# A two-layer hybrid trunk in split fp32: later and larger loads in the down products, their differences on VectorE, and small constants made later

## The chip, the cores and the metric

The kernel runs on one core of a Trainium2 chip. The metric is the device time of one execution in microseconds. The engines are TensorE (PE; its weight loads are listed as PEld), VectorE (DVE), ScalarE (ACT), GpSimd (POOL) and SyncE (SP), which issues every DMA in one ordered queue. Each engine works through its own instructions in the order in which the program lists them, and waits there for semaphores of the others.

## The reference, cut to what matters

Two layers, sequence and width 1024, a hidden width of 4096, all in float32. Layer 0 mixes by dilated window attention, layer 1 by a gated linear recurrence (HGRN2).

```python
def reference(x, ...):
    lbs = forget_lower_bounds(lb_logits)          # softmax and cumulative sum over layers, for HGRN2
    for i in range(2):
        y = dilated_attention_mixer(x, ...) if i == 0 else hgrn2_mixer(x, ..., lbs[i])
        x = layer_norm(ALPHA * x + y, ln_mix_g[i], ln_mix_b[i])
        y = jnp.square(jax.nn.relu(x @ ffn_w_up[i])) @ ffn_w_down[i]     # up: 1024x4096, down: 4096x1024
        x = layer_norm(ALPHA * x + y, ln_ffn_g[i], ln_ffn_b[i])
    return x
```

## The kernel before

**Products.** A float32 operand is split into a high and a low part (`split`: ACT copies it into the type fp32r that PE multiplies, DVE subtracts this from the operand to get the low part), and every product is high x high + high x low + low x high: three matmuls of 128x128 by 128x512. Large products are done in a scheme of the Strassen kind with seven block products instead of eight, numbered i = 1 to 7; each needs sums or differences of blocks as operands and is added to some of the output blocks.

**Stages in time**, by the trace: attention to about 1040 us, its output product and LayerNorm to 1100, up product of layer 0 to 1433, down product to 1768, HGRN2 to 2130, its output product to 2220, up product of layer 1 to 2544, down product to 2866, and the last LayerNorm.

**Up product.** It writes seven left operands for the down product (`hd[i - 1, j]`, 16 tiles of 128x512 each) to DRAM: the squared ReLU of the blocks and their sums S1 to S4. In the last pair of rows these sums (`upa` to `upd`, lines L1131 to L1146) stand on DVE between the first splits of the down product.

**Down product (in `ffn`).** `steps` lists (i, j, quarters): the block products in the order 1, 6, 7, 5, 4, 2, each of 16 steps j, and in each step 12 matmuls (four quarters of 128 rows, three matmuls each). Block product 3 comes last and in three passes over its 16 steps: quarters 0 and 1, then quarter 2, then quarter 3, so that LayerNorm of finished rows runs beside the rest. A turn of the loop calls `load_down(n + 8)`, `product_down(n)`, `split_down(n + 2)` and `after(n)`, which adds results and issues pieces of LayerNorm. Instructions of this loop are placed by a scheduler; a split may stand at most five steps ahead of its product (`HOLD`).

- `load_down` fetches the left tile (`hd`) and, where needed, the right block (`w_down`), 256 KB each, into one slot `dr` of 512 KB; the `U` pool has 50 such slots. For i = 1 three tiles come: left, `top[:, L]`, and `top[:, R]` into `held(3, j)`.
- `split_step` makes the parts `dS` (left) and `dT` (right). The right operands of later products are differences. They are made ahead in the slots `held(n, j)`: POOL makes `held(1, j)` in i = 1 (L1213), the difference of i = 4 in place (L1215), and one of two in i = 6 (L1222); DVE makes the other (L1223).
- In block product 3 the left tile is `d3`, 128x256 or 128x128, loaded step by step into the three buffers of a small pool (tag `p`); its parts are `d3s`, again in three buffers.

**LayerNorm** works on `z`: statistics and scaling on DVE and ACT, an add of the bias on POOL (L212) in layer 0, and in layer 0 a store to `x3d` and transposes on PE (L221).

**Attention.** Turn n multiplies `H` (split weights) with `xh`, `xl` (split x transposed; also its differences xT). Eviction is `e`, L685 on. At n = 11 `constants()` also loads and copies `bsel` (L451), which is read first by the mixing of head groups, near 270 us. `hgrn_consts()` comes in the program behind the attention's output product; its instructions (names `hc_`, 28 on DVE of 128x8) need only `lb_logits`, and the scheduler puts them at the very start.

Of the kernel before, what the change touches and what calls it, by code (L numbers as in the profile page):

```python
# [9 lines left out]
F32 = mybir.dt.float32  # L10
# [33 lines left out]
HOLD = 5  # L44
LOADDN = 8
SPLITDN = 2
LOADW = 8
SPLITW = 5
UNIT0 = 3
# [11 lines left out]
def trunk_kernel(  # L61
# [72 lines left out]
    def split(raw, hi, lo):  # L134
        act(hi, raw, AF.Copy)  # L135
        nc.vector.tensor_sub(lo, raw, hi.bitcast(F32))  # L136
# [180 lines left out]
        return t  # L317


    def attention(pre):  # L320
        cosT = U("cosT")
        sinT = U("sinT")
        units = [(pr, g) for pr in range(NPAIR) for g in GORD]
# [121 lines left out]
        def constants():  # L445
            nc.sync.dma_start(cosT, cos_t)
            nc.sync.dma_start(sinT, sin_t)
            nc.sync.dma_start(mask, masks)
            selw = wp.tile([P, 512], F32, name="selw", tag="p")[:, :NG * P]
            nc.sync.dma_start(selw, bsel)  # L450
            act(sel, selw, AF.Copy)  # L451
            nc.gpsimd.memset(frow.bitcast(F32), 0.0)
# [304 lines left out]
        for n in range(len(seq)):  # L757
            gi, i, j = seq[n]
            load_w(n + LOADW)
            if j == 0 and n // 3 < 6:  # L760
                get_T(n // 3 + 1, 1)
            if j == 1 and n // 3 >= 5:
                get_T(n // 3 + 2, 0)
            if j == 2 and n // 3 >= 5:
                get_T(n // 3 + 2, 1)
            if n == 11:
                constants()
            if n == len(seq) - 2 * PREA - 3:
# [12 lines left out]
            if n % 21 == 14:  # L781
                last = gi == len(groups) - 1
                base = n + 7
                work = [unit_work(gi, a, base) for a in range(2)]
                for a in range(2):
                    adds, rope_of, core, stats, mix = work[a]
                    steps = [f for t in range(2) for f in (lambda rope_of=rope_of, t=t: rope_of(t),
                                                           lambda adds=adds, t=t: adds[t][0](),
                                                           lambda adds=adds, t=t: adds[t][1]())]
                    if last:  # L790
                        both = [lambda f=f: (f[0](), f[1]()) for f in (steps[1:3], steps[4:6])]
                        tail.append(([steps[0], both[0], steps[3], both[1]], core, stats, mix))
                        continue
                    for k, f in zip(ROPES[a], steps):
                        at(base + k, f)
                    for k, f in enumerate(core):
                        at(base + UNIT0 + OFFS[a][k], f)
                    for k, f in zip(STATS[a], stats):
                        at(base + k, f)
                    for k, f in zip(MIX[a], mix):  # L800
                        at(base + k, f)
                if last:
                    for a in range(2):
                        for k, f in list(zip(ROPES0[a], tail[a][0])):
# [202 lines left out]
    def ffn(li, xf, late, res, gB_ap, bB_ap, last, pre=None):  # L1007
# [146 lines left out]
        rows_, ops, hold, keepT = {}, {}, {}, {}  # L1154

        def held(n, j):
            if (n, j // 2) not in hold:
                hold[n, j // 2] = U("hold")
            return hold[n, j // 2][:, (j % 2) * 512:(j % 2) * 512 + 512]

        def load_down(n):
            if n >= len(steps):
                return
            i, j, qs = steps[n]
            top, bot = w_down[li, j], w_down[li, j + NP]
            if i == 3:
                c = slice(qs[0] * P, (qs[-1] + 1) * P)
                t = wp.tile([P, 512], F32, name="d3", tag="p")[:, :len(qs) * P]
                nc.sync.dma_start(t, hd[i - 1, j][:, c])
                r = None  # L1170
                if qs == PASS[0]:
                    r = U("dr3")[:, L]
                    nc.sync.dma_start(r, bot[:, R])
                rows_[n] = t, r
                return
            two = U("dr")
            t, r = two[:, L], two[:, R]
            nc.sync.dma_start(t, hd[i - 1, j])
            if i == 1:
                nc.sync.dma_start(r, top[:, L])  # L1180
                nc.sync.dma_start(held(3, j), top[:, R])
# [7 lines left out]

        def split_down(n):  # L1190
            if n >= len(steps):
                return
            first = len(nc.cur_bb.bb.instructions)
            split_step(n)
            if n - HOLD in begun:
                for i in list(nc.cur_bb.bb.instructions)[first:]:
                    tc.add_manual_dep(i, begun[n - HOLD], mybir.DependencyInfo(
                        mybir.DependencyClass.NoSync, mybir.DependencyReason.DATA), reason="hold")

        def split_step(n):  # L1200
            i, j, qs = steps[n]
            t, r = rows_.pop(n)
            if i == 3:
                w = len(qs) * P
                S_ = wp.tile([P, 512], F32R, name="d3s", tag="pts")[:, :2 * w]
                split(t, S_[:, 0:w], S_[:, w:2 * w])
                if r is not None:
                    keepT[j] = parts_of(r, "dT3")
                ops[n] = S_, keepT[j]
                return  # L1210
            S_ = parts_of(t, "dS")
            if i == 1:
                g.tensor_sub(held(1, j), held(3, j), r)  # L1213
            elif i == 4:
                g.tensor_sub(r, r, held(2, j))  # L1215
            elif i == 5:
                r = held(1, j)
            elif i == 7:
                r = held(3, j)
            elif i == 6:  # L1220
                t1, t2, t3 = held(1, j), held(2, j), held(3, j)
                g.tensor_sub(t2, r, t1)  # L1222
                v.tensor_sub(t3, r, t3)  # L1223
                r = t2
            ops[n] = S_, parts_of(r, "dT")

        cur = {}

        def product_down(n):
            i, j, qs = steps[n]  # L1230
            S_, T_ = ops.pop(n)
# [6 lines left out]
            w = len(qs) * P  # L1238
            for n_, q in enumerate(qs):
                h, l = S_[:, n_ * P:(n_ + 1) * P], S_[:, w + n_ * P:w + (n_ + 1) * P]  # L1240
                nc.tensor.matmul(o[q], h, T_[:, L], start=begin, stop=False, skip_group_check=True)  # L1241
                if n not in begun:
                    begun[n] = list(nc.cur_bb.bb.instructions)[-1].name
                nc.tensor.matmul(o[q], h, T_[:, R], start=False, stop=False, skip_group_check=True)  # L1244
                nc.tensor.matmul(o[q], l, T_[:, L], start=False, stop=end, skip_group_check=True)  # L1245
# [129 lines left out]
        for n in range(len(steps)):  # L1375
            load_down(n + LOADDN)
            product_down(n)
            split_down(n + SPLITDN)
            after(n)
        order.__exit__()  # L1380
        return xn, []
# [78 lines left out]
    def hgrn(xs, late, consts, pre, gw):  # L1460
# [101 lines left out]
        for hd in range(8):  # L1562
# [61 lines left out]
            for i in range(3):  # L1624
# [15 lines left out]
    oN, fill = attention(pr.pre_steps)  # L1640
    xf, late = outproj_ln(pr, oN, fill, lambda t: x[t * P:(t + 1) * P, :],
                          ln_mix_g[0], ln_mix_b[0], x1d)
    hc = hgrn_consts()
    gw = GateW()
    xs, late = ffn(0, xf, late, x1d, ln_ffn_g[0], ln_ffn_b[0], False, lambda: gw.prefetch(0))
    pr = Out(w_hgrn_out, "h", 1)
# [81 lines left out]
```

## Time and profile before

| | |
|---|---|
| Times of three runs | 2872.73, 2873.05, 2877.30 us; median 2873.05 |
| Profiled execution | 2876.54 us, of which the span from first to last instruction is 2874.7 |
| Mean granted PE clock | 0.993 of full speed |
| Busy | PE 2797.4 us (97%), DVE 2085.0 (73%), ACT 1453.8 (51%), POOL 306.0 (11%) |
| DMA engines | 51% busy, 485 MB moved |
| POOL, line L1213 | 32 subtractions of 128x512, 56.3 us, 1767 ns each |
| DVE, line L136, dS | 192 low parts of 128x512, 169.6 us, 883 ns each |

Rows of a timeline give start, duration, engine, line, operation, written and read tiles, shapes, and in brackets how long the engine had stood idle and what released it. Rows of waits give the waiting engine and line, what it waited for, the sum in us, how often, and the longest. Rows of windows give, for a stretch, its length, the busy time and instructions of PE, PEld, DVE, ACT and POOL, the granted clock, the DMA engines' share and GB/s. Starts count from the first instruction.

### The profile page before, as it was taken

What the parts mean: (1) busy time and instruction counts of PE and PEld (TensorE: products, weight loads), DVE (VectorE), ACT (ScalarE), POOL (GpSimd) and SP (SyncE); (2) the same over time, 40 slices, a digit from 0 to 9 for tenths busy, and PEclk for the clock granted to TensorE, in tenths of its full rate; (3) what the DMA queues carried; (4) which work ended last, traced back from release to release, by engine and by line L of the source; (5) the groups of instructions that cost most, each with busy time, mean ns of one, the idle gap of its engine ahead of it and who ended that gap; (6) DMA issues with size and microseconds to landing.
All of it is one profiled execution on the core that took longest, in us unless ns stands there. A gap on an engine that the chain in (4) does not pass through costs nothing. (4 is left out here: it accounts for less than half of the span.)

```text
span 2874.7 us, 40257 instructions
## 1 busy us (share of the span) xinstructions
PE 2797.4 (97%) x14152; PEld 2235.7 (78%) x14152; DVE 2085.0 (73%) x3766; ACT 1453.8 (51%) x3137; POOL 306.0 (11%) x163
## 2 busy tenths in 40 slices
PE   7999999999999989999999999999999999999998
PEld 6777777777777767888878886778877788878885
DVE  7768777777787777786696786564667687678776
ACT  5555555555555455544444445454553644444433
POOL 0000000000000003000160511110101200042400
PEclk9999999999999999999999999999999999999999
DMA  7766665666667423564574733001132365484643
GB/s 269 264 199 192 192 198 176 207 217 199 198 200 222 134 80 143 172 216 145 204 254 144 259 123 121 30 30 59 59 118 103 127 220 177 147 315 148 221 159 113
DMA packets 206218, 485.28 MB, mean 169 GB/s; under 512 B 30656, under 2 KB 44992, under 8 KB 206016
## 3 DMA queue, kind: packets, MB, share of 16 engines
q1 hardware_dynamic: 206016, 482.72, 51.0%
q8 instruction: 111, 1.82, 0.3%
q14 instruction: 91, 0.75, 0.1%
HBM read 362.82 MB, written 94.24 MB: 159 GB/s over the span
## 5 line engine op out<-in xcount | busy, mean ns | idle before, releaser
L662 PE MATMUL pmm<-xh,H 128*128 128x512 f32 x1008 | 407.4, 404 | 16.0 <-ACT H L430 9.2
L664 PE MATMUL pmm<-xh,H 128*128 128x512 f32 x1008 | 395.8, 393 | 1.0 <-DVE H L438 1.0
L663 PE MATMUL pmm<-xl,H 128*128 128x512 f32 x1008 | 395.5, 392 | 0.0
L662 PEld LDWEIGHTS pmm<-xh,H 128*128 128x128 f32 x1008 | 190.8, 189 | 56.1 <-ACT H L430 9.2
L664 PEld LDWEIGHTS pmm<-xh,H 128*128 128x128 f32 x1008 | 190.1, 189 | 43.3 <-DVE H L438 1.7
L663 PEld LDWEIGHTS pmm<-xl,H 128*128 128x128 f32 x1008 | 190.8, 189 | 36.7
L510 ACT ACTIVATE p<-p,stats 128x128 f32<-128x128 f32 (+1 forms) x384 | 168.4, 442 | 99.9 <-DVE stats L507 99.5
L1241 PE MATMUL pdy<-dT,dS 128*128 128x512 f32 x512 | 199.2, 389 | 0.0
L1244 PE MATMUL pdy<-dT,dS 128*128 128x512 f32 x512 | 199.2, 389 | 0.0
L1245 PE MATMUL pdy<-dT,dS 128*128 128x512 f32 x512 | 199.2, 389 | 0.0
L212 POOL TENSOR_TENSOR z<-z,bB 128x1024 f32<-128x1024 f32 x24 | 58.6, 2444 | 1294.5 <-ACT z L211 1287.7
L136 DVE TENSOR_TENSOR dS<-dr,dS 128x512 fp32r<-128x512 f32 x192 | 169.6, 883 | 12.2 <-ACT dS L135 12.2
L135 ACT ACTIVATE dS<-dr 128x512 fp32r<-128x512 f32 x192 | 120.0, 625 | 111.6 <-PE pdy L1245 43.7
L507 DVE CUSTOM_DVE_ANT_0 p<-s,mask 128x128 f32<-128x128 f32 (+1 forms) x384 | 113.6, 348 | 66.0 <-PE s L496 58.4
L169 PE MATMUL pmm<-f0nh,wh 128*128 128x512 f32 x384 | 153.2, 399 | 0.7 <-ACT wh L135 0.7
L171 PE MATMUL pmm<-f0nh,wl 128*128 128x512 f32 x384 | 149.9, 390 | 0.0
L170 PE MATMUL pmm<-f0nl,wh 128*128 128x512 f32 x384 | 149.7, 390 | 0.0
L1213 POOL TENSOR_TENSOR hold<-hold,dr 128x512 f32<-128x512 f32 x32 | 56.3, 1767 | 548.8 <-DMA hold<-in_w_down_dram 540.3
L523 ACT ACTIVATE pts<-ppt 128x256 f32<-128x256 f32 (+1 forms) x192 | 85.5, 474 | 56.9 <-PE ppt L520 55.1
L1065 ACT ACTIVATE H<-wc 128x512 fp32r<-128x512 f32 x128 | 77.2, 625 | 73.3 <-DVE wc L1058 44.0
L136 DVE TENSOR_TENSOR dT<-dr,dT 128x512 fp32r<-128x512 f32 x128 | 111.4, 875 | 2.5 <-ACT dT L135 1.8
L1244 PEld LDWEIGHTS pdy<-dT,dS 128*128 128x128 f32 x512 | 96.1, 188 | 20.0
(395 smaller groups left out, 7133.4 us busy)
## 6 DMA issues: line engine op xcount, KB each, us to landing
xh<-xtd SPq DMA_DIRECT2D x110, 512.0 KB
xl<-xtd SPq DMA_DIRECT2D x110, 512.0 KB
dr<-hd SPq DMA_DIRECT2D x192, 256.0 KB
dr<-in_w_down_dram SPq DMA_DIRECT2D x160, 256.0 KB
rot<-e SPq DMA_DIRECT2D x192, 128.0 KB
wa<-in_w_up_dram SPq DMA_DIRECT2D x48, 512.0 KB
wb<-in_w_attn_dram SPq DMA_DIRECT2D x36, 512.0 KB
wa<-in_w_attn_dram SPq DMA_DIRECT2D x33, 512.0 KB
```

Of the source, the lines that this page charges most:

```text
L135: act(hi, raw, AF.Copy)
L136: nc.vector.tensor_sub(lo, raw, hi.bitcast(F32))
L169: nc.tensor.matmul(o, wh[:, k], xs.h(k), start=k == 0, stop=False)
L170: nc.tensor.matmul(o, wh[:, k], xs.l(k), start=False, stop=False)
L171: nc.tensor.matmul(o, wl[:, k], xs.h(k), start=False, stop=k == NK - 1)
L510: act(p[:, h, :n], p[:, h, :n], AF.Exp, bias=sS[:, 0, h, b:b + 1], scale=-1.0, accum_out=sS[:, 1, h, b:b + 1])
L662: nc.tensor.matmul(o, wh, hi[k // 2][:, c], start=begin and k == 0, stop=False, skip_group_check=True)
L663: nc.tensor.matmul(o, wh, lo[k // 2][:, c], start=False, stop=False, skip_group_check=True)
L664: nc.tensor.matmul(o, wl, hi[k // 2][:, c], start=False, stop=end and k == 3, skip_group_check=True)
L1241: nc.tensor.matmul(o[q], h, T_[:, L], start=begin, stop=False, skip_group_check=True)
L1244: nc.tensor.matmul(o[q], h, T_[:, R], start=False, stop=False, skip_group_check=True)
L1245: nc.tensor.matmul(o[q], l, T_[:, L], start=False, stop=end, skip_group_check=True)
```

## The change

It has three parts. In the down products the right block `top[:, R]` of i = 1 is loaded with step j + 4, and the subtractions of POOL go to DVE. The left tiles of block product 3 come in loads of 512 KB into `U` slots (four steps of pass 1, eight of passes 2 and 3), and in passes 2 and 3 one split of 256 columns serves two steps and is issued up to four steps ahead. In attention, the bsel part of `constants()` moves from n = 11 to n = 30 and `hgrn_consts()` to n = 36, where DVE's and PE's orders are those of the program.

```diff
+SPLIT3 = 4
+SHIFT = 4
...
-        def constants():
...
+        def constants2():
             selw = wp.tile([P, 512], F32, name="selw", tag="p")[:, :NG * P]
             nc.sync.dma_start(selw, bsel)
             act(sel, selw, AF.Copy)
...
+            if n == 30:
+                constants2()
+            if n == 36:
+                hc.append(hgrn_consts())
...
             top, bot = w_down[li, j], w_down[li, j + NP]
+            if 0 <= n - SHIFT < NP:
+                nc.sync.dma_start(held(3, n - SHIFT), w_down[li, n - SHIFT][:, R])
             if i == 3:
-                t = wp.tile([P, 512], F32, name="d3", tag="p")[:, :len(qs) * P]
-                nc.sync.dma_start(t, hd[i - 1, j][:, c])
+                w = len(qs) * P
+                js = 1024 // w
+                if j % js == 0:
+                    many[qs] = U("d3")
+                    nc.sync.dma_start(many[qs].rearrange("p (j c) -> p j c", c=w),
+                                      hd[i - 1, j:j + js, :, qs[0] * P:qs[0] * P + w].rearrange("j p c -> p j c"))
+                t = many[qs][:, j % js * w:min(j % js * w + 256, 1024)]
...
             if i == 1:
-                nc.sync.dma_start(r, top[:, L])
-                nc.sync.dma_start(held(3, j), top[:, R])
+                nc.sync.dma_start(held(1, j), top[:, L])
...
-                S_ = wp.tile([P, 512], F32R, name="d3s", tag="pts")[:, :2 * w]
-                split(t, S_[:, 0:w], S_[:, w:2 * w])
+                S_ = wp.tile([P, 512], F32R, name="d3s", tag="pts")
+                split(t, S_[:, 0:256], S_[:, 256:512])
...
+                if len(qs) == 1:
+                    rows_.pop(n + 1)
+                    ops[n + 1] = S_[:, P:256], S_[:, 256 + P:512], keepT[j + 1]
...
             if i == 1:
-                g.tensor_sub(held(1, j), held(3, j), r)
+                r = held(1, j)
             elif i == 4:
-                g.tensor_sub(r, r, held(2, j))
+                v.tensor_sub(r, r, held(2, j))
...
-                g.tensor_sub(t2, r, t1)
+                v.tensor_sub(t2, r, t1)
...
+            if 0 <= n - SHIFT + 1 < NP:
+                a = n - SHIFT + 1
+                v.tensor_sub(held(1, a), held(3, a), held(1, a))
...
+            if n + SPLIT3 < len(steps) and len(steps[n + SPLIT3][2]) == 1:
+                split_down(n + SPLITDN + 1)
+                split_down(n + SPLIT3)
...
+    hc = []
+    oN, fill = attention(pr.pre_steps, hc)
...
-    hc = hgrn_consts()
+    hc = hc[0]
```

How this moves instructions shows at three places (numbers behind names tell buffers apart; the new kernel's lines are 2 to 22 higher). ACT at the start, before: two splits of an x block (`xh_157`, `xh_158`), the copy of bsel, the splits of xT2, the first eviction.

```order
9 L135 ACTIVATE xh_157<-x11_110 128x1024
10 L135 ACTIVATE xh_158<-x11_112 128x1024
11 L451 ACTIVATE bsel_95<-selw_415 128x384
12 L135 ACTIVATE xh_173<-xT2_169 128x1024
13 L135 ACTIVATE xh_174<-xT2_170 128x1024
14 L685 ACTIVATE e_194<-pmm_181 128x512
15 L430 ACTIVATE H_196<-wa_108 128x512
```

And in the changed kernel:

```order
9 L137 ACTIVATE xh_157<-x11_110 128x1024
10 L137 ACTIVATE xh_158<-x11_112 128x1024
11 L137 ACTIVATE xh_173<-xT2_169 128x1024
12 L137 ACTIVATE xh_174<-xT2_170 128x1024
13 L689 ACTIVATE e_194<-pmm_181 128x512
14 L432 ACTIVATE H_196<-wa_108 128x512
```

The copy of bsel has left this place, and nothing has come in. The second place is DVE at the seam of layer 0's up and down products, before: the up product's last sums (`upb`, `upd`, `upc`, `upa`) among the first splits of the down product.

```order
2120 L1131 TENSOR_TENSOR upb_13290<-pup_13370,upc_13338 128x512
2121 L136 TENSOR_TENSOR dS_13392<-dr_13244,dS_13392 128x512
2122 L136 TENSOR_TENSOR dT_13397<-dr_13244,dT_13397 128x512
2123 L1137 TENSOR_TENSOR upd_13412<-pup_13348,upb_13290 128x512
2124 L1146 TENSOR_TENSOR upd_13412<-upa_13262,upd_13412 128x512
2125 L136 TENSOR_TENSOR dS_13422<-dr_13273,dS_13422 128x512
2126 L136 TENSOR_TENSOR dT_13426<-dr_13273,dT_13426 128x512
2127 L1146 TENSOR_TENSOR upc_13338<-upd_13412,upc_13338 128x512
2128 L1146 TENSOR_TENSOR upb_13290<-upc_13338,upa_13262 128x512
2129 L1146 TENSOR_TENSOR upa_13262<-upb_13290 128x512
2130 L136 TENSOR_TENSOR dS_13456<-dr_13297,dS_13456 128x512
2131 L136 TENSOR_TENSOR dT_13461<-dr_13297,dT_13461 128x512
```

In the changed kernel (L1245 is the subtraction that POOL made; `hold_13339` holds the right blocks that are loaded later):

```order
2120 L1139 TENSOR_TENSOR upb_13288<-pup_13367,upc_13334 128x512
2121 L138 TENSOR_TENSOR dS_13390<-dr_13244,dS_13390 128x512
2122 L138 TENSOR_TENSOR dT_13393<-hold_13246,dT_13393 128x512
2123 L1145 TENSOR_TENSOR upd_13408<-pup_13345,upb_13288 128x512
2124 L1245 TENSOR_TENSOR hold_13246<-hold_13339,hold_13246 128x512
2125 L1154 TENSOR_TENSOR upd_13408<-upa_13261,upd_13408 128x512
2126 L138 TENSOR_TENSOR dS_13418<-dr_13272,dS_13418 128x512
2127 L138 TENSOR_TENSOR dT_13421<-hold_13246,dT_13421 128x512
2128 L1154 TENSOR_TENSOR upc_13334<-upd_13408,upc_13334 128x512
2129 L1245 TENSOR_TENSOR hold_13246<-hold_13339,hold_13246 128x512
2130 L1154 TENSOR_TENSOR upb_13288<-upc_13334,upa_13261 128x512
2131 L1154 TENSOR_TENSOR upa_13261<-upb_13288 128x512
```

Two subtractions stand in the chain of sums and splits, and the third step's `dS` and `dT` follow in the next two rows. The same triple `dS`, `dT`, L1245 repeats for the steps behind. The third place is SP in the last block product of layer 1, before: loads of quarter tiles among the stores of the finished rows.

```order
1402 L1169 DMA d3_25033<-hd1_86 128x128
1403 L209 DMA out_0_dram<-z_23846 128x512 x2
1404 L1169 DMA d3_25041<-hd1_86 128x128
1405 L1169 DMA d3_25049<-hd1_86 128x128
1406 L1169 DMA d3_25073<-hd1_86 128x128
1407 L209 DMA out_0_dram<-z_23848 128x512 x2
1408 L1169 DMA d3_25081<-hd1_86 128x128
```

In the changed kernel, passes 2 and 3 together:

```order
1341 L1181 DMA d3_24765<-hd1_86 128x8x128
1342 L1181 DMA d3_24859<-hd1_86 128x8x128
1343 L1181 DMA d3_24913<-hd1_86 128x8x128
1344 L1181 DMA d3_24968<-hd1_86 128x8x128
1345 L211 DMA out_0_dram<-z_23718 128x512 x2
1346 L211 DMA out_0_dram<-z_23720 128x512 x2
1347 L211 DMA out_0_dram<-z_23722 128x512 x2
```

All four loads stand ahead of the stores. In layer 0 they do not: SP has there, in the changed kernel,

```order
893 L1181 DMA d3_15806<-hd0_85 128x8x128
894 L1181 DMA d3_15900<-hd0_85 128x8x128
895 L1296 DMA x3d_89<-z_14719 128x1024
896 L1296 DMA x3d_89<-z_14721 128x1024
897 L1181 DMA d3_15997<-hd0_85 128x8x128
898 L1181 DMA d3_16087<-hd0_85 128x8x128
```

where the last two are those of pass 3, behind the stores of two rows of `z` to `x3d`.

More of the change, by code (lines that the diff above doesn't have):

```diff
@@ L317, in parts_of, with attention @@
         return t
-    def attention(pre):
+    def attention(pre, hc):
         cosT = U("cosT")
@@ L1153, in ffn @@
         steps += [(3, j, qs) for qs in PASS for j in range(NP)]
-        rows_, ops, hold, keepT = {}, {}, {}, {}
+        rows_, ops, hold, keepT, many = {}, {}, {}, {}, {}
         def held(n, j):
@@ L1165, in load_down @@
             top, bot = w_down[li, j], w_down[li, j + NP]
+            if 0 <= n - SHIFT < NP:
+                nc.sync.dma_start(held(3, n - SHIFT), w_down[li, n - SHIFT][:, R])
             if i == 3:
-                c = slice(qs[0] * P, (qs[-1] + 1) * P)
-                t = wp.tile([P, 512], F32, name="d3", tag="p")[:, :len(qs) * P]
-                nc.sync.dma_start(t, hd[i - 1, j][:, c])
+                w = len(qs) * P
[5 more added lines that the diff above has]
+                t = many[qs][:, j % js * w:min(j % js * w + 256, 1024)]
                 r = None
@@ L1191, in split_down @@
             if n >= len(steps):
+                return
+            if n in ops:
                 return
@@ L1203, in split_step @@
             if i == 3:
-                w = len(qs) * P
-                S_ = wp.tile([P, 512], F32R, name="d3s", tag="pts")[:, :2 * w]
-                split(t, S_[:, 0:w], S_[:, w:2 * w])
+                S_ = wp.tile([P, 512], F32R, name="d3s", tag="pts")
+                split(t, S_[:, 0:256], S_[:, 256:512])
                 if r is not None:
                     keepT[j] = parts_of(r, "dT3")
-                ops[n] = S_, keepT[j]
+                ops[n] = S_[:, 0:256], S_[:, 256:512], keepT[j]
+                if len(qs) == 1:
+                    rows_.pop(n + 1)
+                    ops[n + 1] = S_[:, P:256], S_[:, 256 + P:512], keepT[j + 1]
                 return
@@ L1221, in split_step @@
                 t1, t2, t3 = held(1, j), held(2, j), held(3, j)
-                g.tensor_sub(t2, r, t1)
+                v.tensor_sub(t2, r, t1)
                 v.tensor_sub(t3, r, t3)
                 r = t2
-            ops[n] = S_, parts_of(r, "dT")
+            ops[n] = S_[:, L], S_[:, R], parts_of(r, "dT")
+            if 0 <= n - SHIFT + 1 < NP:
+                a = n - SHIFT + 1
+                v.tensor_sub(held(1, a), held(3, a), held(1, a))
         cur = {}
@@ L1230, in product_down @@
             i, j, qs = steps[n]
-            S_, T_ = ops.pop(n)
+            sh, sl, T_ = ops[n]
             if j == 0 and i in (1, 5):
@@ L1237, in product_down @@
             begin, end = j == 0 and i in (1, 5, 6, 2), j == NP - 1 and i in (1, 2, 3, 4)
-            w = len(qs) * P
             for n_, q in enumerate(qs):
-                h, l = S_[:, n_ * P:(n_ + 1) * P], S_[:, w + n_ * P:w + (n_ + 1) * P]
+                h, l = sh[:, n_ * P:(n_ + 1) * P], sl[:, n_ * P:(n_ + 1) * P]
                 nc.tensor.matmul(o[q], h, T_[:, L], start=begin, stop=False, skip_group_check=True)
@@ L1639, in trunk_kernel @@
     pr = Out(w_attn_out, "a", 0)
-    oN, fill = attention(pr.pre_steps)
+    hc = []
+    oN, fill = attention(pr.pre_steps, hc)
     xf, late = outproj_ln(pr, oN, fill, lambda t: x[t * P:(t + 1) * P, :],
                           ln_mix_g[0], ln_mix_b[0], x1d)
-    hc = hgrn_consts()
+    hc = hc[0]
     gw = GateW()
```

## The prediction

> **What bounds the kernel now.** I read the busy times first.
>
> ```profile
> PE 2797.4 (97%) x14152; PEld 2235.7 (78%) x14152; DVE 2085.0 (73%) x3766; ACT 1453.8 (51%) x3137; POOL 306.0 (11%) x163
> ```
>
> TensorE (PE) is busy for 97% of the 2874.7 us span, and the change leaves its instructions alone. Time can therefore come only from the 77 us in which PE is idle and from stretches at a lower clock. The idle stretches and their waits, read next, lie in three places that the edits touch: the start, the first steps of both down products, and the last product of both.
>
> The timeline of the start (start, us, engine, in brackets the idle time and its releaser):
>
> ```profile
> 19.38 2.35 DVE L349 TENSOR_TENSOR xT<-x,xT 128x1024 f32<-128x1024 f32 x2
> ...
> 23.87 0.52 ACT L451 ACTIVATE bsel<-selw 128x384 fp32r<-128x384 f32 x1 [8.12 <-DMA selw<-in_bsel_dram]
> ...
> 24.30 1.99 ACT L135 ACTIVATE xh<-xT 128x1024 fp32r<-128x1024 f32 x2
> ...
> 26.19 0.58 ACT L685 ACTIVATE e<-pmm 128x512 f32<-128x512 f32 x1
> ...
> 26.82 0.80 PE L662 MATMUL pmm<-xh,H 128*128 128x512 f32 x1 [6.82 <-ACT e L685]
> 27.41 0.63 PE L663 MATMUL pmm<-xl,H 128*128 128x512 f32 x1
> ...
> 30.40 0.63 PE L664 MATMUL pmm<-xh,H 128*128 128x512 f32 x1
> ```
>
> ScalarE (ACT) works in order. Its copy of bsel waits 8.12 us for a small load; the splits of xT and the eviction e stand behind it, and PE waits 6.82 us for e. After that pause matmuls follow at (30.40 − 27.41)/7 = 0.427 us.
>
> The windows by stage give, left to right, PE, weight load, VectorE (DVE), ACT and GpSimd (POOL), then clock, DMA share and rate. The rows are the down product's first product (i=1), its second (i=6) and third (i=7) in layer 0:
>
> ```profile
> 1433.40:1482.80 49.40, 46.23 (x191) 36.85 (x192) 47.58 (x46) 22.49 (x39) 38.92 (x20) 0.97 0.98 354
> 1482.80:1526.30 43.50, 43.50 (x193) 36.02 (x192) 36.73 (x47) 22.35 (x41) 13.04 (x8) 1.00 0.33 102
> 1526.30:1569.80 43.50, 43.50 (x193) 36.02 (x193) 24.93 (x41) 19.17 (x33) 0.00 (x0) 1.00 0.50 152
> ```
>
> All hold the same 192 matmuls. i=6 and i=7 take 43.5 us with PE full; i=1 takes 49.4, so 5.9 us are lost, and there DVE is busy for 47.58 us with only 46 instructions. Its timeline tells why:
>
> ```profile
> 1436.14 0.69 DVE L1146 TENSOR_TENSOR upd<-upa,upd 128x512 f32<-128x512 f32 x1 [1.36 <-ACT upd L1094]
> ...
> 1436.27 1.72 POOL L1213 TENSOR_TENSOR hold<-hold,dr 128x512 f32<-128x512 f32 x1 [0.94 <-DMA hold<-in_w_down_dram]
> ...
> 1436.75 1.78 DVE L136 TENSOR_TENSOR dS<-dr,dS 128x512 fp32r<-128x512 f32 x1
> ...
> 1439.04 1.85 POOL L1213 TENSOR_TENSOR hold<-hold,dr 128x512 f32<-128x512 f32 x1 [1.06 <-DMA hold<-in_w_down_dram]
> ...
> 1439.77 1.67 DVE L1146 TENSOR_TENSOR upb<-upc,upa 128x512 f32<-128x512 f32 x1
> ...
> 1442.09 0.69 DVE L136 TENSOR_TENSOR dS<-dr,dS 128x512 fp32r<-128x512 f32 x1
> ...
> 1442.69 0.68 DVE L136 TENSOR_TENSOR dT<-dr,dT 128x512 fp32r<-128x512 f32 x1
> ...
> 1443.43 0.50 PE L1244 MATMUL pdx<-dT,dS 128*128 128x512 f32 x1 [1.90 <-DVE dT L136]
> ```
>
> A DVE instruction that meets a POOL subtraction takes 1.67 to 1.78 us, and one that meets none 0.68 to 0.69; back to back they start 0.60 apart (1442.09, 1442.69). PE waits for the end of this DVE chain, the low part dT of the third step.
>
> **The change part by part.**
>
> *Start.* Both small-constant blocks leave. The two xT splits can now begin while DVE makes xT (its two subtractions end at 19.38 + 2.35 = 21.73). The second split takes half of 1.99 us, 1.0, then e 0.58: PE resumes at 23.4 instead of 26.8, a gain of **3.4 us**. A pause of 3.4 us is left, and I keep the slow clock behind it (the layer-1 rows below show it after 1.39 us idle). Without it 8 to 10 matmuls gain 0.2 each, 2.1 at most, so the bounds are 2.5 and 5.5.
> The Trainium skill (TensorE: Matmul & The Clock Gate, Part 1) lets the clock fall after an idle window of about 3.4 us, which runs free. By that rule the shorter pause may keep full speed; the 1.39 us below speak against it.
>
> *The block at product 36.* It is 28 DVE instructions of this size in one run, with three waits for ACT between:
>
> ```profile
> L1404 DVE TENSOR_TENSOR hc_e<-hc_e,hc_den 128x8 f32<-128x8 f32 x2 | 0.2, 162 | 0.0
> ...
> L1402 DVE RECIPROCAL hc_den<-hc_den 128x8 f32<-128x8 f32 x1 | 0.2, 197 | 0.0
> 107.00:152.00 45.00, 44.74 (x267) 34.49 (x266) 29.02 (x76) 28.41 (x83) 0.00 (x0) 1.00 0.61 195
> ```
>
> 28 x 0.165 = 4.6 us, 0.7 for the copy of cm, and up to a microsecond for each wait: 6 to 9 us in which the evictions' subtractions, the score work L507 and the weights' low parts H queue on DVE. Products 30 to 40 have PE full (44.74 of 45.00) and DVE at 29.02, so 16 us are free and the block fits, but in one piece. I take **+0.5**, bounds 0 and 4. The bsel load and copy at product 30 have no reader nearby: 0.
>
> *First product of the down products.* The ACT copies that start the chain (upd, 1436.14) do not move. In the new order nine DVE instructions run from there to the low part dT of the third step: upd, dS, dT, upc, one subtraction, upb, upa, dS, dT. Eight starts 0.60 apart and the last at 0.68 end at 1436.14 + 4.8 + 0.7 = 1441.6, and PE goes 0.06 later: 1441.7 instead of 1443.43, **1.7 us**. The other new subtraction there falls into DVE's idle 1.36. Layer 1 has the same chain:
>
> ```profile
> 2544.96 1.76 DVE L136 TENSOR_TENSOR dT<-dr,dT 128x512 fp32r<-128x512 f32 x1
> ...
> 2546.77 0.71 PE L1244 MATMUL pdx<-dT,dS 128*128 128x512 f32 x1 [1.39 <-DVE dT L136]
> 2547.27 0.63 PE L1245 MATMUL pdx<-dT,dS 128*128 128x512 f32 x1
> ...
> 2555.97 0.50 PE L1244 MATMUL pdx<-dT,dS 128*128 128x512 f32 x1 [1.84 <-DVE dT L136]
> ```
>
> There the first dT is slow too (1.76, not 0.68), which moves everything behind it by another 1.1: **2.8 us**. In both layers PE still pauses for about 1.4 us, and I let the slow clock behind this pause stand. Together **4.5**, bounds 0 (the waits are only renamed) and 7.7 (that slow clock, 8 matmuls x 0.2 a layer, goes too). The steps behind are safe: with POOL silent, DVE has three instructions a step, 1.8 of 2.72 us. i=6 has four, 2.4 of 2.72; its window would hold about 59 x 0.60 = 36 of 43.5 us, so 0, at worst 3 a layer. POOL loses its 96 subtractions of the down products. SP issues the same loads, each right block four steps later, so that 20 loads and not 24 come ahead of the first product; nothing else is passed by them.
>
> The Trainium skill (GPSIMD Engine Reference, 8. Key points) says that GpSimd shares its SBUF interfaces with VectorE and contends with instructions of two SBUF inputs: the trace agrees (1.78 against 0.68).
>
> *Last product, layer 1.*
>
> ```profile
> 2813.16:2866.40 53.24, 47.53 (x193) 34.61 (x191) 36.34 (x89) 21.30 (x60) 0.00 (x0) 1.00 0.33 99
> ```
> ```profile
> ACT d3s L135 <- DMA d<-hd: 15.9, 18, 2.1
> ...
> PE pdx L1241 <- ACT d3s L135: 3.2, 7, 0.9
> PE pdx L1245 <- DVE d3s L136: 2.4, 4, 0.9
> ```
> ```profile
> SPq L1169 <- DVE d3s L136: 30.9, 29, 8.6
> ```
>
> 192 matmuls take 53.24 us, 9.7 over 43.5. The loads go round three buffers: SP waits for the split that frees one (29 times), the split for the load, PE for the split. In the new order all four loads of passes 2 and 3 are issued before any output store, and a split serves two steps, up to four steps ahead. I leave 1.1 us for splits that stand behind LayerNorm work on DVE: **8.6**, bounds 6 and 9.7. The tail behind the last matmul stays.
>
> *Last product, layer 0.*
>
> ```profile
> 1700.40:1768.30 67.90, 62.38 (x286) 47.30 (x285) 52.02 (x114) 36.42 (x97) 7.99 (x4) 1.00 0.42 133
> ```
> ```profile
> 1733.59 4.73 POOL L212 TENSOR_TENSOR z<-z,bB 128x1024 f32<-128x1024 f32 x2 [46.05 <-ACT z L211]
> ```
> ```profile
> 1733.74 4.73 DVE L136 TENSOR_TENSOR d3s<-d,d3s 128x128 fp32r<-128x128 f32 x2 [0.40 <-ACT d3s L135]
> ```
>
> PE is idle for 67.90 − 62.38 = 5.5 us, and matmuls beside a pause start late, which may add half as much. But here LayerNorm's adds on POOL hold DVE for 4.73 us, and those stay; a read-ahead of four short steps (4 x 3 matmuls x 0.227 = 2.7 us) covers half. The loads of pass 3 stand on SP behind two stores of z, which wait for these adds (end 1738.3); with two to three microseconds to land and the split, pass 3 starts near 1742. I take **4**, bounds −1 and 8.
>
> The sum is −3.4 + 0.5 − 4.5 − 8.6 − 4.0 = −20.0. The profiled execution took 2876.54 us (span 2874.7 and 1.84 around it), 3.5 over the median of 2873.05. It becomes 2856.5, the median **2853.0**. About 0.2%, 5.7 us, is what a measurement of this kernel can tell from no change.
>
> **The rivals.**
>
> *Slow by itself (slower).* If DMA traffic (0.98 busy in i=1), and not POOL, makes DVE instructions long, 16 more of them at the mean of 47.58/46 = 1.03 us make i=1 DVE-bound: 64 us for 49.4, +14.7 a layer; in i=6, 59 at 36.73/47 = 0.78 are 46.1 for 43.5, +2.6. Twice 17.3 less the other 15.5 is +19: 2892. It decides from a mean of 0.80 on (62 instructions in 49.4 us) and outweighs the rest from 0.92. Against it: 0.68 at 1442.69 amid the same traffic, and long ones only beside POOL. 0.07.
>
> *Layer 0 gives nothing.* The stores ahead of pass 3's loads cost what the ring cost, 4 us: 2857. For it: the 4.73 us on POOL. 0.12.
>
> *The seam's waits are renamed.* The new subtraction sits inside the chain, and each waits in order for a right block issued two loop turns (5.4 us) earlier:
>
> ```profile
> 1438.21 0.41 SPq L1181 DMA_DIRECT2D hold<-in_w_down_dram  x1
> ...
> 1443.11 1.41 POOL L1213 TENSOR_TENSOR hold<-hold,dr 128x512 f32<-128x512 f32 x1 [2.21 <-DMA hold<-in_w_down_dram]
> ```
>
> Issue to use is 4.9 us while the DMA engines are full, so the margin is thin; dS and dT of the next steps, and PE, stand behind. It takes the 4.5 us, once per layer since loads catch up: 2857.5. 0.10.
>
> *The constants in attention block DVE* for 9 us where a score or an eviction is due: +8 with the clock, 2861. Against it, the free 16 us. 0.05.
>
> *The clock stays up after the start* (by that rule): 2.1 more, 2851. 0.05.
>
> **How the numbers follow.** My forecast has 0.55. With the four milder rivals 0.87 lies over 5.7 us faster. Where three shortfalls meet (4 + 4.5 + 8 of 20 gone) little over 3 us is left: 0.06 within 0.2%. Slower 0.07. The range leaves out that meeting and the slower rival: upward it takes two shortfalls (4 + 4.5) and the bounds of start and constants (0.9 + 3.5), 13 us, 2866; downward all upper bounds (2.1 + 0.5 + 3.2 + 1.1 + 4 = 10.9), 2842.
>
> **What would show it.** PE's pause near 20 us should be about 3.4; POOL nearly absent between 1420 and 1530, with DVE's dS and dT at 0.60 to 0.70; the i=1 windows near 47 us; 192 matmuls of layer 1's last product in 44 to 45; a pause in layer 0's pass 3 beside POOL's adds. DVE instructions of 1 us or more in i=1 without POOL, PE waits for H near 130 us, or an i=6 window over 43.5 would prove me wrong.

## The result and the profile after

The changed kernel takes 2856.49 us in the median of four runs (2854.79 to 2856.82), against 2873.41 before (four runs, 2872.73 to 2877.30): ratio 0.9937, 95% interval 0.9920 to 0.9954, 17 us less. Repeated later on another chip the ratio was 0.9937 again (0.9922 to 0.9952). The forecast was 2853.0. The profiled execution has a span of 2854.6 us, 20.1 less than before. The profiled execution of before (2876.54 us) stood 3.1 over its median and that of after (2856.82 us) 0.3, which is most of the difference between 20 and 17; the forecast had let both stand equally far above. One execution of a later run, that with two edits, was disturbed (4454.81 us): it is left out of the times below, and no trace of that run is read.

The total came out as the sum said, the parts did not. This table gives what each place changed in TensorE's time (minus is time saved), from the start times of the same matmul (counted through both traces) at the ends of each place:

| Place | Forecast, us | In the traces, us |
|---|---|---|
| Pause near 20 us | −3.4 | −3.6 |
| Constants in attention (77 to 124 us) | +0.5 | +3.7 |
| First down product, layer 0 | −1.7 | −3.9 |
| First down product, layer 1 | −2.8 | −5.0 |
| Last down product with its LayerNorm, layer 0 | −4.0 | −0.5 |
| Last down product, layer 1, with the tail behind it | −8.6 | −9.3 |
| Elsewhere | 0 | −1.5 |

"Elsewhere" is an earlier first matmul (0.7), one pause of 1.0 near 764 us that comes in some executions, that of before among them, and stages that the change doesn't touch. In the last row the last matmul comes 9.8 us earlier, and the tail behind it is 0.5 longer.

The pause near 20 us is 3.5 us now, as TensorE's wait there shows (the numbers are the sum, how often, and the longest):

```profile
PE pmm L666 <- ACT e L689: 3.5, 1, 3.5
```

The page's busy times, and the windows of the first down product, its follower (layer 0), the first down product of layer 1 and the last one of layer 1, in the order of columns used above:

```profile
PE 2789.4 (98%) x14152; PEld 2235.3 (78%) x14152; DVE 2053.8 (72%) x3830; ACT 1448.4 (51%) x3105; POOL 122.6 (4%) x67
```
```profile
1431.67:1477.39 45.72, 44.53 (x193) 35.96 (x193) 40.62 (x66) 22.88 (x39) 0.00 (x0) 1.00 1.02 364
1477.39:1520.91 43.52, 43.52 (x194) 36.05 (x192) 35.13 (x58) 22.71 (x41) 0.00 (x0) 1.00 0.42 126
2539.03:2584.75 45.72, 44.55 (x193) 35.96 (x193) 40.63 (x66) 22.79 (x39) 0.00 (x0) 1.00 1.02 369
2802.35:2845.90 43.55, 43.55 (x193) 35.86 (x191) 33.91 (x73) 18.37 (x45) 0.00 (x0) 1.00 0.27 79
```

GpSimd's subtractions are gone from the down products. VectorE has 66 instructions in i=1 instead of 46 and is busy for less time (40.62 instead of 47.58 us). i=6 stays at 43.5 us with 58 instructions. The last product of layer 1 has no idle time left.

The timeline of the seam in layer 0 after the change:

```profile
1434.39 0.69 DVE L1154 TENSOR_TENSOR upd<-upa,upd 128x512 f32<-128x512 f32 x1 [0.77 <-ACT upd L1102]
1435.00 0.69 DVE L138 TENSOR_TENSOR dS<-dr,dS 128x512 fp32r<-128x512 f32 x1
...
1436.81 0.69 DVE L1245 TENSOR_TENSOR hold<-hold 128x512 f32<-128x512 f32 x1
1437.41 0.69 DVE L1154 TENSOR_TENSOR upb<-upc,upa 128x512 f32<-128x512 f32 x1
...
1440.08 0.50 PE L1263 MATMUL pdx<-dT,dS 128*128 128x512 f32 x1 [0.69 <-DVE dT L138]
```

Every instruction of the chain takes 0.69 us, the new subtraction (L1245) among them, and TensorE's pause is 0.69 us instead of 1.90. No slow clock follows it: the matmuls behind it start about 0.23 us apart.

What was not forecast stands in attention, at product 30:

```profile
115.58 0.39 PE L668 MATMUL pmm<-xh,H 128*128 128x512 f32 x1
116.01 0.60 ACT L697 ACTIVATE e<-pmm 128x512 f32<-128x512 f32 x1 [2.12 <-PE pmm L668]
116.50 0.59 ACT L695 ACTIVATE e<-pmm 128x512 f32<-128x512 f32 x1
116.98 1.03 ACT L550 ACTIVATE og<-o 128x512 f32<-128x512 f32 x1
...
118.06 0.66 PE L539 MATMUL o<-pts,vn 128*64 128x128 f32 x8 [2.09 <-ACT og L550]
```

TensorE waits for ScalarE's copy of og, and this stands behind an eviction (L697) of the product that TensorE has only just finished. Behind this pause matmuls start 0.427 us apart for a while, which with the pause makes up the 3.7 us. In the trace of before the order on ScalarE is the other one (L546 is the copy of og, L693 the eviction):

```profile
118.02 0.59 ACT L691 ACTIVATE e<-pmm 128x512 f32<-128x512 f32 x1
118.50 1.09 ACT L546 ACTIVATE og<-o 128x512 f32<-128x512 f32 x1
119.35 0.67 ACT L430 ACTIVATE H<-wc 128x512 fp32r<-128x512 f32 x1
120.24 0.60 ACT L693 ACTIVATE e<-pmm 128x512 f32<-128x512 f32 x1 [0.22 <-PE pmm L664]
```

In layer 0's last product the waits of TensorE have new names. Before, most was spent waiting for split tiles:

```profile
PE pdx L1245 <- DVE d3s L136: 4.3, 5, 1.7
PE lnpt L221 <- POOL z L212: 1.4, 1, 1.4
```

Now transposes (lnpt) wait for z and for f0nl (the low part of the transposed rows), and one wait is for a split (d3s) that waits for its load:

```profile
PE lnpt L223 <- POOL z L214: 3.2, 3, 1.5
PE pdx L1260 <- ACT d3s L137: 2.3, 1, 2.3
PE lnpt L223 <- DVE f0nl L234: 1.5, 3, 0.7
```

SP's timeline there, and GpSimd's:

```profile
1731.94 2.68 SPq L1296 DMA_DIRECT2D x3d<-z  x2
1734.71 1.47 SPq L1181 DMA_DIRECT2D d<-hd  x2
```
```profile
1729.55 4.72 POOL L214 TENSOR_TENSOR z<-z,bB 128x1024 f32<-128x1024 f32 x2 [47.66 <-ACT z L213]
```

The second store is issued when the second add has ended (1729.55 + 4.72 = 1734.27), and only then the loads of pass 3.

### The profile page after: what moved, and what is told of

The parts are those of the page before. It is cut to its first block, busy times and chain, and to the rows that moved or that the text cites. A ratio compares the mean times of both kernels' runs of the same rounds, so it can differ in the third digit from the quotient of the medians.

```text
span 2854.6 us, 39893 instructions
## 1 busy us (share of the span) xinstructions
PE 2789.4 (98%) x14152; PEld 2235.3 (78%) x14152; DVE 2053.8 (72%) x3830; ACT 1448.4 (51%) x3105; POOL 122.6 (4%) x67
## 4 chain that ended last, share of the span: by engine, by line
PE 90%; DVE 4%; ACT 2%; DMA 1%; issue 1%; POOL 0%; SPq 0%; DVEq 0%; POOLq 0%; ACTq 0%
PE pmm L666 8%; PE pmm L668 8%; PE pmm L667 8%; PE pup L1114 7%; PE pup L1112 7%; PE pup L1113 7%; PE pdy L1264 4%; PE pdy L1260 4%; PE pdy L1263 4%; PE pmm L171 3%; PE s L500 3%; PE pdx L1263 3%; PE pdx L1264 3%; PE pdx L1260 3%; PE pmm L173 3%; PE pmm L172 3%
## 5 line engine op out<-in xcount | busy, mean ns | idle before, releaser
L138 DVE TENSOR_TENSOR dS<-dr,dS 128x512 fp32r<-128x512 f32 x192 | 135.1, 703 | 16.5 <-ACT dS L137 16.5
L137 ACT ACTIVATE dT<-hold 128x512 fp32r<-128x512 f32 x128 | 80.0, 625 | 69.5 <-DVE hold L1239 28.8
L1263 PEld LDWEIGHTS pdy<-dT,dS 128*128 128x128 f32 x512 | 96.1, 188 | 20.0
L1264 PEld LDWEIGHTS pdy<-dT,dS 128*128 128x128 f32 x512 | 96.1, 188 | 20.0
```

## The experiments

Each starts from the changed kernel, where nothing else is said. Ratios are to the kernel before on the same chip, with 0.9937 for the changed kernel; 0.001 is 2.9 us.

**Constants one turn later.**

```diff
-            if n == 30:
+            if n == 31:
```

> The bsel part of the small constants stands one turn later, at product 31 instead of 30; nothing else changes. Theory (order on ScalarE): at product 30 the scheduler had put an eviction that waits for a later product (e, L697) ahead of the copy of og (L550), for which TensorE waits; with product 31 og stands ahead again. So the pause of 2.1 us near 116 us goes and with it the 1.6 us of slow clock behind it: about 3.5 us less than the changed kernel, near 2853. Rival (the constants' own instructions on VectorE or ScalarE cost this time there): the pause stays or moves by a product, 2856 to 2857.

Ratio 0.9923 (0.9908 to 0.9938), 4 us less in the point estimate. TensorE's waits between 100 and 130 us, here and in the changed kernel:

```profile
PE ppt L524 <- ACT p L514: 0.5, 1, 0.5
```
```profile
PE o L539 <- ACT og L550: 2.1, 1, 2.1
```

The pause is gone, as the theory said, so it was the order on ScalarE: one turn of the loop decides where the scheduler puts the eviction. Between 77 and 124 us 2.7 of the 3.7 us come back. The remaining 1.0 is a new wait of 0.5 us and its surroundings. Another 1.6 us of the gain were not expected and are not the edit's: in this run no slow clock follows the pause at 20 us.

**Subtractions back on GpSimd.**

```diff
-                v.tensor_sub(r, r, held(2, j))
+                g.tensor_sub(r, r, held(2, j))
...
-                v.tensor_sub(t2, r, t1)
+                g.tensor_sub(t2, r, t1)
...
-                v.tensor_sub(held(1, a), held(3, a), held(1, a))
+                g.tensor_sub(held(1, a), held(3, a), held(1, a))
```

> The three subtractions of the down products are given back to GpSimd; the later loads and everything else stay as changed. Theory (GpSimd's subtractions stretch VectorE's): VectorE's dS, dT and sums of 1.7 us come back at the seam, the first product takes 48.5 to 49.5 us a layer again instead of 45.6, the slow clock behind the pause returns, and the time is 6 to 8 us over the changed kernel, 2862 to 2865. Rival (the later right blocks, four loads fewer ahead of the first product, brought the gain): the first product stays near 45.6 us, 2856 to 2857.

Ratio 0.9993 (0.9984 to 1.0002): nearly all is lost, twice what was expected, and elsewhere. The windows of i=1 and i=6 in layer 0, and TensorE's wait in i=6:

```profile
1430.89:1477.37 46.48, 44.83 (x193) 35.86 (x193) 45.05 (x43) 23.00 (x39) 32.03 (x20) 1.00 1.01 362
1477.37:1528.72 51.35, 45.90 (x194) 37.20 (x193) 42.36 (x50) 22.91 (x41) 27.48 (x13) 0.93 0.35 106
```
```profile
PE pdy L1263 <- DVE dT L138: 5.4, 1, 5.4
```

VectorE's instructions are long again beside GpSimd's (42.36 us in i=6 for 50 of them against 35.13 for 58). But i=1 takes only 46.5 us, not the expected 48.5 to 49.5, since one instruction of the chain at the seam is hit (1.68 us) and no more: with the later loads GpSimd comes to its subtractions later. It ends those of i=1 at 1474.8 us (before the change at 1467.2), so that its subtractions of i=6 (L1239) come late too, eight of them in one row:

```profile
1474.78 13.57 POOL L1239 TENSOR_TENSOR hold<-dr,hold 128x512 f32<-128x512 f32 x8
```

TensorE waits 5.4 us there, at a mean clock of 0.93, and i=6 takes 7.8 us more in layer 0 and 8.1 in layer 1. So the later loads without the change of engine move the loss and don't remove it.

**Loads not later.**

```diff
-            if 0 <= n - SHIFT < NP:
-                nc.sync.dma_start(held(3, n - SHIFT), w_down[li, n - SHIFT][:, R])
...
                 nc.sync.dma_start(held(1, j), top[:, L])
+                nc.sync.dma_start(held(3, j), top[:, R])
```

> The right blocks of the first down product are loaded with their own step again, as before the change (24 loads ahead of the first product and not 20); the subtractions stay on VectorE. Theory (the engine alone counts): the first product stays at 45.6 us within 0.5, time 2856 to 2857. Rival (the DMA engines, full in this stage, limit it): the left tiles and the stores of the up product come later, ScalarE waits for dr, the first product takes 47 us or more, and the time is 3 to 7 us over the changed kernel.

Ratio 0.9937 (0.9921 to 0.9954), that of the changed kernel.

```profile
1428.87:1475.26 46.39, 44.53 (x192) 35.95 (x193) 39.46 (x66) 22.70 (x39) 0.00 (x0) 1.00 1.03 374
```

i=1 is 0.7 us longer (46.39 against 45.72), a little over the 0.5 that the theory allowed, and far from the rival's 3 to 7 us in the time. The engine brings 3.3 us of the 3.9 in layer 0 and 4.2 of the 5.0 in layer 1; the later loads bring 0.7 us a layer, which is under what the times can tell.

**All loads of passes 2 and 3 with the first** (`fetch` is the changed kernel's load, made a function).

```diff
+                if qs == PASS[1] and j == 0:
+                    for q_ in PASS[1:]:
+                        for j_ in range(0, NP, js):
+                            fetch(q_, j_)
```

> In the last down product all four loads of passes 2 and 3 are issued together with the first of pass 2, so that in layer 0 they stand ahead of the stores of z that wait for GpSimd's adds. Theory (the loads behind the stores took what the read-ahead gave): TensorE's pause of 2.3 us at the start of pass 3 and the slow clock around it (1.8) go: 2 to 4 us less than the changed kernel, 2852 to 2854. Rival (the transposes of rows that wait for GpSimd's adds hold TensorE in order anyway): the pause turns into longer waits of the transposes, under 1 us is won, 2855.5 to 2857.

Ratio 0.9922 (0.9907 to 0.9937). TensorE's waits in layer 0's last product:

```profile
PE lnpt L223 <- POOL z L214: 3.6, 3, 1.4
PE pdx L1266 <- ACT dT L137: 1.7, 3, 1.0
PE lnpt L223 <- DVE f0nl L234: 1.6, 1, 1.6
```

The wait for d3s is gone. The transposes still wait for z (3.6 us, 3.2 in the changed kernel), and the wait for dT has grown from 0.7 to 1.7 us. By the starts of the same matmuls the place gains 2.1 us, of which 0.9 are left when HGRN2 runs. Of the 3.9 us that the span is shorter, 1.4 come from the start (no slow clock there in this run) and 1.6 from the stretch between attention's end and the first down product, which the edit doesn't touch. Both theories hold in part, and the gain of the edit itself is nearer to the rival's.

**LayerNorm's end on VectorE for four row tiles.**

```diff
+        if dve:
+            for i in range(2):
+                c = slice(i * 512, i * 512 + 512)
+                nc.vector.scalar_tensor_tensor(z[:, c], z[:, c], w[:, 3:4], bB[:, c], op0=ALU.mult, op1=ALU.add)
+            return
         act(z, z, AF.Copy, scale=w[:, 3:4])
         nc.gpsimd.tensor_add(z, z, bB)
...
-            ln_math(z[t], norm["g"], norm["b"])
+            ln_math(z[t], norm["g"], norm["b"], dve=t < 4)
```

> In layer 0's last down product the LayerNorm of the first four row tiles ends like that of the last layer: two scalar_tensor_tensor of VectorE (0.75 us each by the profile) instead of a copy on ScalarE and the add on GpSimd (about 1 + 2.4 us). The rest is the changed kernel. Theory (GpSimd's adds hold both VectorE and the rows that TensorE transposes): the transposes' waits for z (1.3, 0.4 and 1.5 us) shrink to under 1 us in all, the stores of z and with them the loads of pass 3 come 2 us earlier, and 3 to 5 us are won against the changed kernel. Rival (VectorE is short of time there): its splits d3s come later and the gain is under 1 us or a loss.

Ratio 0.9907 (0.9893 to 0.9922), 8.6 us less, more than expected. TensorE's waits there:

```profile
PE lnpt L228 <- DVE f0nl L239: 1.4, 2, 0.7
PE pdx L1265 <- ACT dT L137: 0.7, 2, 0.5
```

The three waits for z and the wait for the load are gone, and so is the slow clock; the waits for f0nl stay. The place is 7.5 us shorter in the trace. So LayerNorm's end on GpSimd was behind the waits for z, and through the stores behind that for the load. The edit takes away ScalarE's copy together with the add, and makes the end shorter (two instructions of 0.75 us instead of about 1 + 2.4 us); what the copy cost by itself is not shown.

**The three edits together**, and **without the earlier loads**:

> The three edits together: small constants one turn later (product 31), all loads of passes 2 and 3 with the first of pass 2, LayerNorm's end of the four row tiles on VectorE. If their gains lie in different places they add: 3.5 to 4 and 4 measured for the first two, and what the third adds once the loads are early (1 to 3, the transposes' waits alone): 8.5 to 11 us under the changed kernel, a ratio to before of 0.9900 to 0.9908. If the third one only brings the loads forward, it adds nothing to the second: 0.9909 to 0.9914.

> Small constants one turn later and LayerNorm's end of layer 0's four row tiles on VectorE, with the loads of passes 2 and 3 left as the change has them. Theory (the loads stood late only because the stores ahead of them waited for GpSimd's adds): nothing is missing against the kernel with all three edits, ratio to before 0.9895 to 0.9906. Rival (early loads count by themselves): 1 to 4 us more than with all three, 0.9905 to 0.9915.

Ratios 0.9901 (0.9887 to 0.9916) and 0.9905 (0.9889 to 0.9922; four runs between 2847.19 and 2848.95 us). The first lies where the sum of the three gains put it. The second lies where the ranges of theory and rival overlap; the earlier loads add nothing that can be told once the adds are off GpSimd.

**A split for every step.**

```diff
-                t = many[qs][:, j % js * w:min(j % js * w + 256, 1024)]
+                t = many[qs][:, j % js * w:j % js * w + w]
...
-                split(t, S_[:, 0:256], S_[:, 256:512])
-                if len(qs) == 1:
-                    rows_.pop(n + 1)
-                    ops[n + 1] = S_[:, P:256], S_[:, 256 + P:512], keepT[j + 1]
+                split(t, S_[:, 0:w], S_[:, 256:256 + w])
...
-            if n + SPLIT3 < len(steps) and len(steps[n + SPLIT3][2]) == 1:
-                split_down(n + SPLITDN + 1)
-                split_down(n + SPLIT3)
```

> The last down product keeps the loads of 512 KB, but in passes 2 and 3 every step has its own split of 128 columns again, issued two steps ahead as before the change. Theory (the ring of three small load buffers was the bound): the last product of layer 1 stays within 2 us of the changed kernel's (near 44 us), and the time within 3 us of it. Rival (the number of splits and their read-ahead were the bound): half or more of the 9 us of layer 1 and the little of layer 0 come back, time 5 to 9 us over the changed kernel.

Ratio 0.9941 (0.9924 to 0.9957). The last product of layer 1:

```profile
2803.50:2848.80 45.30, 44.75 (x193) 35.47 (x191) 35.44 (x89) 21.58 (x61) 0.00 (x0) 1.00 0.26 76
```

45.3 us against 43.55 with paired splits and 53.24 before: the theory holds. The large loads bring 8 us, the paired and earlier splits 1.7. Whether it is the size of the loads, their own buffers or their place ahead of the output stores that brings the 8 us was not separated.

**bsel at product 11 again.**

```diff
-            if n == 30:
+            if n == 11:
```

> The bsel part of the small constants goes back to product 11; the VectorE block hgrn_consts stays at product 36. Theory (ScalarE's copy of bsel, waiting for its load, held the start): TensorE's pause near 20 us is 6 to 6.8 us again, 3 us more than changed; the reordering at product 30 is gone too, 3.5 us less: in all within 1 us of the changed kernel. Rival (VectorE's block for HGRN2, waiting for its load at 24 us, held the start): the pause stays near 3.5 us, and the time is 3 to 4 us under the changed kernel.

Ratio 0.9936 (0.9921 to 0.9951), within 1 us of the changed kernel, as the theory had it. The wait at the start:

```profile
PE pmm L666 <- ACT e L689: 7.1, 1, 7.1
```

So ScalarE's copy of bsel held the start, and moving the block of VectorE alone to product 36 brings nothing there. It costs nothing either: between 77 and 166 us, with the block at 127 to 134, this kernel runs like the one before within 0.1 us.

**The subtraction out of the chain**, on top of the two edits (product 31, LayerNorm):

```diff
-            if 0 <= n - SHIFT + 1 < NP:
-                a = n - SHIFT + 1
+            if 0 <= n - SHIFT < NP:
+                a = n - SHIFT
                 v.tensor_sub(held(1, a), held(3, a), held(1, a))
+                tc.add_manual_dep(list(nc.cur_bb.bb.instructions)[-1], begun[a + 2], mybir.DependencyInfo(
+                    mybir.DependencyClass.NoSync, mybir.DependencyReason.DATA), reason="hold")
```

> As the run before, and the new subtraction of block a in the first down product is held back until two steps later, so that at the seam of the up and down products VectorE's chain of sums and splits has none of them. Theory (TensorE waits there for the end of this chain, one instruction of 0.60 us start to start longer through the subtraction): the pause of 0.7 us at the third step shrinks to about 0.1 in both layers, 1.0 to 1.3 us in all, ratio 0.0004 lower. Rival (ScalarE's copies of upd set the end of the chain, the subtraction fills a gap): the pause stays at 0.6 to 0.7 us.

Ratio 0.9896 (0.9882 to 0.9911), the fastest: 2845.04 us against 2875.04 on its chip.

```profile
1429.44:1474.68 45.24, 44.54 (x192) 35.95 (x193) 38.45 (x64) 22.79 (x39) 0.00 (x0) 1.00 1.02 367
```

TensorE's waits for low parts dT at this seam, in the changed kernel and here:

```profile
PE pdx L1263 <- DVE dT L138: 1.0, 2, 0.7
```
```profile
PE pdx L1270 <- DVE dT L138: 0.5, 2, 0.3
```

i=1 takes 45.24 us instead of 45.72, 0.5 less in each layer, and the pause at the third step is 0.23 us instead of 0.69 (0.17 instead of 0.67 in layer 1). The chain sets the pause, though the gain is under what the times can tell.

The changed kernel was run beside it with this expectation:

> The changed kernel once more, on the chip of the two runs beside it: a ratio to before of 0.993 to 0.995.

It gave 0.9937.

## Why the prediction was right, and where not

**Start.** Right: 3.5 us of pause were left, and the copy of bsel was its cause.

**The constants.** Wrong by 3.2 us. The step that failed is "the bsel load and copy at product 30 have no reader nearby: 0". It weighed who waits for these instructions, not what their presence does to the scheduler's order of ScalarE, whose order attention leaves free. The swapped pair (eviction L697 ahead of the copy of og, L550) stands in the order of the changed kernel's ScalarE, and could have been read there. The 3.7 us are inside the bounds of 0 to 4, but those were meant for another cause. The block of VectorE at product 36, for which the 0.5 and a rival were meant, costs nothing.

**First down products.** The mechanism was right: GpSimd's subtractions stretch VectorE's instructions, and with the engine changed (and the loads not) the gain is there. The chain was sized well: from the first matmul of i=1 to the one that ends the pause 8.41 us, forecast 8.28, before 10.01. What was mis-sized is the pause itself, 0.7 us and not 1.4, since TensorE reaches it later than the forecast had it: in the new order it runs four matmuls on the high part of the third step's dT ahead of the wait and not one, three more of 0.227 us. Behind 0.7 us no slow clock came, in any run. Pause and clock together make 2.2 us a layer, 4.4 in all, and the 8.9 us of the two layers lie outside the bounds of 0 to 7.7.

**Rivals of these products.** DMA traffic doesn't stretch VectorE's instructions: 0.68 to 0.69 us with the DMA engines full (share 1.02). The loads come in time for the chain at the seam, and i=6 holds its four instructions a step (43.52 us).

**Last product, layer 1.** Right: the window is 9.7 us shorter, and the 1.1 us left for splits behind LayerNorm were not needed. The tail, taken as unchanged, gave 0.5 back.

**Last product, layer 0.** The rival "layer 0 gives nothing" came true, with 0.5 us. The term's own sentence named the stores and adds ahead of the loads; the sizing erred in taking a wait of pass 3 for the only loss. Transposes stand in TensorE's order too and wait for the same adds, and a slow clock followed. The experiment on LayerNorm's end shows its add and copy, taken together, as the cause: without them 7.5 us go.

The errors, −0.2, +3.2, −4.4, +3.5, −0.7 and −1.5 elsewhere, cancelled to 0.1 in the span. That is luck, and that the sum was right says little of its parts. The median of 2856.5 us even lies nearer to two of the rivals, layer 0 giving nothing (2857) and the renamed waits (2857.5), than to the forecast; only the traces by place tell that the first of them came true and the second did not.

## What to carry to other kernels

Before work is moved to GpSimd because it is idle, look at which VectorE instructions run beside it: here a free engine cost 7.5 us through the one that was needed (the gain without the later loads), and the end of LayerNorm on it another 7.5. When small instructions are moved, compare the order of every engine that a scheduler orders, not only the place where they land. And a total that comes out right should still be split by place, since the places tell what to do next.

## What the runs showed of the hardware

How long a pause is doesn't by itself decide whether the slow clock follows, the state in which matmuls of 128x512 start 0.427 us apart and not 0.227. After the start's pause of 3.28 us one run kept full speed, after 3.27 us another did not (windows from 20 to 32 us of the run with LayerNorm's end on VectorE and of the one with three edits; the clock is the third column from the right):

```profile
20.00:32.00 12.00, 9.12 (x40) 7.57 (x41) 11.89 (x18) 6.16 (x10) 0.00 (x0) 1.00 0.61 237
```
```profile
20.00:32.00 12.00, 8.73 (x31) 6.91 (x31) 11.59 (x16) 5.99 (x9) 0.00 (x0) 0.86 0.64 249
```

Over twelve runs, pauses of 2.99 to 3.28 us there were followed by it once in six, and pauses of 3.42 us and more always (six). At other places shorter pauses were followed by it too: 1.39, 1.84 and 1.90 us at the seams before the change, and 2.09 at product 30. But 1.38 us at both seams of the run with loads not later kept full speed, and so did 0.7 us always. At the start the slow clock makes 1.6 us between executions (8 matmuls at 0.427 instead of 0.227 us). The Trainium skill (TensorE: Matmul & The Clock Gate, Part 1) has the clock follow activity in windows of 3.4 us that run free. Windows that run free fit the equal pauses with unequal ends; but most of these pauses are shorter than such a window, so the rule fits them only if a window needn't be wholly idle, which no run here tests.

GpSimd held short VectorE instructions here as long as its own: beside two adds of 128x1024 (4.73 us) two subtractions of 128x128 took 4.73 us before the change, and single ones of that size take 0.28 (1730.35 in the same trace).
